# Program order for three engines, borders of stages written out, and six raw weight buffers in a two-layer encoder trunk

## The chip, the cores and the metric

The kernel runs on one core of a Trainium2 chip. The metric is the device time of one execution in microseconds (us); lower is better. Before the change it is 979.01 us, the median of three runs (977.41 to 979.86).

The engines named below are TensorE (PE: matrix products and transposes), VectorE (DVE), ScalarE (ACT), GpSimd (POOL) and SyncE (SP, which here only starts transfers). Each has its own instruction stream; they meet through semaphores.

## The reference, cut to what matters

x is 256 tokens by 1024 features, all in float32. Two layers run one after the other, each with a gated feed-forward block (FFN1), a mixing block ("mix") and a second feed-forward block (FFN2):

```
for l in range(DEPTH):                                   # DEPTH = 2, D_FF = 2816
    x = x + 0.5 * swiglu(rms_norm(x, ffn1_norm[l]), ffn1_w_gate[l], ffn1_w_up[l], ffn1_w_down[l])
    h = rms_norm(x, mix_norm[l])
    qa, ka, va, qb, kb, vb = split(h @ w_in[l])
    out_a = windowed_gqa_sink(qa, ka, va, sink[l], slopes_a)          # 8 heads, window 128
    lam   = exp(sum(lam_q1[l]*lam_k1[l])) - exp(sum(lam_q2[l]*lam_k2[l])) + lam_init
    out_b = rms_norm(differential_attention(qb, kb, vb, lam, slopes_b), diff_subln[l]) * (1 - lam_init)
    x = x + concat([out_a, out_b]) @ w_out[l]
    x = x + 0.5 * swiglu(rms_norm(x, ffn2_norm[l]), ffn2_w_gate[l], ffn2_w_up[l], ffn2_w_down[l])
return rms_norm(x, final_norm)
# swiglu(h, wg, wu, wd) = (silu(h @ wg) * (h @ wu)) @ wd
```

All weights are read from memory once, 167.5 MB in all.

## The kernel before, in words

*Products.* Every float32 product is made of three matmuls in a reduced 32-bit format (fp32r): each operand is split into a high part, rounded to fp32r, and a low part, the rest. The product is xh·whi + xl·whi + xh·wlo, added up in PSUM. `tokens` does this with 128 tokens as the stationary and 512 weight columns as the moving operand (128x512); `narrow` does it with the weights stationary and all 256 tokens moving (128x256).

*Weights.* `specs` is the list of all weight pieces in the order of use, mostly 1 MB each (128 partitions x 4 x 512). `emit_load` makes for one of them the transfer into a raw buffer on SP's queue, the casts on ACT (`whi`, L116) and the differences on DVE (`wlo`, L117). There are three buffers each of raw, whi and wlo. `weights()` hands out the next split weight and emits the loads up to two weights ahead (LOOK = 2); transfer and split of a weight are emitted together, and a transfer waits until the DVE difference that last read its raw buffer is done. The first two weights (gate and up, rows 0 to 511) come in four pieces each. `fine` marks the weights whose splits are cut in four.

*The order of work.* Instructions are emitted in Python in some order, and a scheduler (which plans with a timeline of its own) places them on each engine. PE's matmuls and transposes go through `mm` (L67) and `flip` (L70), which keep them in program order. ACT and DVE are in the scheduler's order, with `urgent()` raising the priority of norm operands, SiLU, the up product, splits of the hidden state and residual adds.

*Norms.* `Norm.pair(j)` transposes two 128-column blocks of x for both token halves (PE, four transposes of 128x128 for each block pair), and `operands` multiplies by the gain and splits the result: high part on ACT (L197), low part on DVE (L198), two of each per pair. `squares` sums x² on ACT (L183); `stats` makes r = 1/rms on DVE and POOL (L204 to L208); r is applied behind the products. The first FFN takes x by `take_x`, the later ones by `Residual.late`, which does what is left of the norm (pairs 2 and 3, squares, stats) inside the first matmul group of the next stage.

*FFN.* The 2816 hidden columns are five groups of 512 and one of 256. One group is: gate products in two halves of the features (k0 = 0, 4), up products in two halves, `hidden` (SiLU on ACT, L402; product with up on DVE, L408), `turn` (transposes of the hidden state of the group before and their split, ACT L336 and DVE L337), and two down products into accumulators that stay in PSUM for the whole FFN. In a full group PE does 144 matmuls of 128x512. `ffn_close` ends an FFN: the last down products are ordered so that columns 0 to 511 are complete first, are added to x (`Residual.add`, L382) and turned for the next norm, while columns 512 to 1023 are still being multiplied.

*Mix.* `first_groups` makes the keys and queries, which is the start of the input projection. Attention follows (lines 540 to 700), then the output projection: `out_part(w, k0, h)` takes two 128-row pieces of w_out from k0 on for column half h. Rows 4 to 7 belong to the differential attention (`oT[2:4]`, split in L682 and L683), rows 0 to 3 to the windowed attention, whose outputs are scaled on DVE (L702) and then transposed and split.

*Constants.* POOL starts the small transfers: the gains of the first norm (`grow1`, L225), then in `attention_constants` the other gains (L278, L279), after an iota and memsets the sinks (L299) and the four lambda vectors (L308), each copied to all 128 partitions. SP's queue starts with the first weights, ACT's with x in four pieces (L228).

Of the kernel before, what the change touches and what calls it, by code (L numbers as in the profile page):

```python
# [27 lines left out]
LOOK = 2  # L28
N_RAW, N_HI, N_LO = 3, 3, 3
N_S4 = 18  # L30
# [3 lines left out]
def trunk(ctx: ExitStack, tc: tile.TileContext, x, n1, g1, u1, d1, nm, w_in, sink,  # L34
          lq1, lk1, lq2, lk2, subln, w_out, n2, g2, u2, d2, nf, out):
    nc = tc.nc
    pe, act, dve, pool, sp = nc.tensor, nc.scalar, nc.vector, nc.gpsimd, nc.sync
# [27 lines left out]
    def mm(*a, **k):  # L65

        tc.keep_in_program_order(pe.matmul(*a, **k))  # L67

    def flip(*a):
        tc.keep_in_program_order(pe.transpose(*a))  # L70

# [4 lines left out]

    specs = []
    loaded = {}
# [7 lines left out]
    def plain(w, c0, n, k0=0, kn=None):  # L86
        src = rows(w, c0, n, k0, kn)
        kn = src.shape[1]
        return (kn, n, lambda t: [(t, src)])

    def emit_load(i):
        kn, n, moves = specs[i]
        raw = wp.tile([P, kn, n], F32, tag="raw", bufs=N_RAW, name=nm_("raw"))
# [4 lines left out]
        for dst, src in moves(raw):  # L98
            if i > 1:
                sp.dma_start(dst, src)  # L100
            else:
                for a, b in zip(cuts, cuts[1:]):
                    sp.dma_start(dst[:, a:b], src[:, a:b])  # L103
                    yield
# [15 lines left out]
    nxt = [0, 0]  # L120

    def weights():
        i = nxt[0]
        nxt[0] += 1
        while i > 1 and nxt[1] <= min(i + LOOK, len(specs) - 1):
            for _ in emit_load(nxt[1]):
                pass
            nxt[1] += 1
        return loaded.pop(i)

    for l in range(DEPTH):
        def ffn_specs(wg, wu, wd):
# [3 lines left out]
            for g in range(1, NGRP):  # L136
                specs.extend(plain(w[l], g * 512, 512, k0, 4) for w in (wg, wu) for k0 in (0, 4))
                specs.extend(down(g - 1, h) for h in range(2))
            for k0 in (0, 4):
                def gu_moves(t, k0=k0, ws=(wg[l], wu[l])):  # L140
                    return [(t[:, :, h * 256:h * 256 + 256], rows(w, FF - 256, 256, k0, 4)) for h, w in enumerate(ws)]
                specs.append((4, 512, gu_moves))
# [10 lines left out]
        for c in range(2):  # L153
# [3 lines left out]
            specs.append((KC, 256, qa_moves))  # L157
# [5 lines left out]
        for k0 in (0, 2):  # L163
# [3 lines left out]
            specs.append((2, D, o_moves))  # L167
# [6 lines left out]
    class Norm:  # L174


        def __init__(self, g0):
            self.g0, self.xs = g0, []
            self.ss = tmp("nss", 2, (P, 2, 4))

        def squares(self, t, c, n):
            j_ = tmp("junk", 2, (P, 512))
            act.activation(j_[:, :n], xk[:, t, c:c + n], AF.Square, accum_out=self.ss[:, t, c // 256:c // 256 + 1])  # L183

        def pair(self, j):
            sl = halves(bank())
            for i in range(2):
                for t in range(2):
                    flip(sl[:, i, t * P:(t + 1) * P], xk[:, t, (2 * j + i) * P:(2 * j + i + 1) * P], ident)
            with urgent():  # L190
                self.operands(j, sl)

        def operands(self, j, sl):
            xs = blk()
            for i in range(2):
                g = gcol[:, self.g0 + 2 * j + i:self.g0 + 2 * j + i + 1]
                self.last_act = act.activation(xs[:, i, 0:S], sl[:, i], AF.Identity, scale=g)  # L197
                self.last = dve.scalar_tensor_tensor(xs[:, i, S:512], in0=sl[:, i], scalar=g, in1=f(xs[:, i, 0:S]),  # L198
                                                     op0=ALU.mult, op1=ALU.subtract)
            self.xs.append(xs)  # L200
# [11 lines left out]
        def spread(self, sl):  # L212
# [4 lines left out]
            mm(sl[:, 0:S], lhsT=ones, rhs=dg, start=True, stop=True)  # L217
# [7 lines left out]
    pool.dma_start(grow1, n1.rearrange("l (k p) -> (l k) p", p=P))  # L225
    early = [emit_load(0), emit_load(1)]
# [4 lines left out]
    nxt[1] = 2  # L231
# [13 lines left out]
    def take_x(k):  # L245

        if k < 4:
            norm.pair(k)
            for e in early * 2 if k < 2 else ():
                next(e)  # L250
        else:
            with tc.issue_after(norm.last_act.ins):
                for t in range(2):
                    for h in range(2):
                        norm.squares(t, h * 512, 512)
            norm.stats()

    grow = const.tile([NG - 16, P], F32, name="grow")
    dist_i = const.tile([P, 512], mybir.dt.int32, name="dist_i")
# [7 lines left out]
    lin = const.tile([P, 4, DEPTH * 64], F32, name="lin")  # L267
    lsum = const.tile([P, 2, DEPTH], F32, name="lsum")
    lpr = const.tile([P, 2, DEPTH * 64], F32, name="lpr")
# [5 lines left out]

    def attention_constants():
        for i, g in enumerate((nm, n2)):
            pool.dma_start(grow[i * 16:(i + 1) * 16], g.rearrange("l (k p) -> (l k) p", p=P))  # L278
        pool.dma_start(grow[32:34], subln)  # L279
# [3 lines left out]

        pool.iota(dist_i, pattern=[[P, 2], [-1, S]], base=0, channel_multiplier=1)
        dflat = distB.rearrange("p a b -> p (a b)")
        aflat = distA.rearrange("p a b -> p (a b)")
        dve.tensor_copy(aflat, dist_i)
# [3 lines left out]


        for c in range(4):
            pool.memset(qscA[0:64, c:c + 1], -0.125 / slopeA[c])
            pool.memset(qscA[64:128, c:c + 1], -0.125 / slopeA[c + 4])
            pool.memset(qscB[:, c:c + 1], -0.125 / slopeB[c])


        pool.dma_start(snk_in, sink.rearrange("l h -> (l h)").partition_broadcast(P))  # L299
        sv = snk_in.rearrange("p (l s c) -> p l c s", l=DEPTH, s=2)  # L300
        for t in range(2):
            for l in range(DEPTH):
                pool.tensor_copy(snk[:, l, :, t, :], sv[:, l])
# [522 lines left out]
```

## Time and profile before

| | us |
|---|---|
| median of 3 runs | 979.01 |
| the profiled execution | 977.06 |
| its span, first to last instruction | 975.3 |
| PE busy | 954.0 |
| DVE busy | 555.4 |
| ACT busy | 475.1 |
| POOL busy | 22.0 |
| granted TensorE clock, mean | 0.998 |
| DMA rate over the span | 173 GB/s |

All durations below come from the one profiled execution. Its own time, 977.06 us, is 1.7 us more than its span and 1.95 us less than the median. The stages follow one another in the span: FFN1 of layer 0 from 0 to about 201 us, mix to 301, FFN2 to 490, FFN1 of layer 1 to 678, mix to 778, FFN2 to 968, and the final norm to 975. "Busy" counts the time in which an instruction of the engine runs; matmuls overlap, so a row of the timeline gives starts, and the distance from start to start is what a matmul costs. In such a row the first number is the start, the second the time to the end of the group, then engine, line and operation, what it writes and reads, its shapes, how many in a row, and in brackets how long the engine was idle before it and who ended that.

### The profile page before, as it was taken

The page shows a single profiled execution, that of the slowest core. Times are in us where ns is not written, and L with a number is a line of the kernel's source. Part 1 is how long each engine was busy: PE and PEld are TensorE (multiplying, and loading weights), DVE is VectorE, ACT ScalarE, POOL GpSimd, SP SyncE. Part 2 cuts the span into 40 slices and gives each one's busy share as a digit, 9 for nine tenths or more (in the row PEclk, how much of TensorE's full clock was granted, in tenths as well). Part 3 has the DMA queues.
Part 4 walks back from the last instruction along what each step waited for, and adds up shares of the span by engine and source line. Part 5 has one row for each costly group of instructions (what it writes and reads, how often), then busy time and mean ns, then how long its engine had stood idle before and what let it go on. Part 6 is the DMA issues. An engine that isn't in the chain of part 4 may idle for free.

```text
span 975.3 us, 12345 instructions
## 1 busy us (share of the span) xinstructions
PE 954.0 (98%) x4940; PEld 808.2 (83%) x4940; DVE 555.4 (57%) x850; ACT 475.1 (49%) x779; POOL 22.0 (2%) x50
## 2 busy tenths in 40 slices
PE   7999999999999999999999999999999999999997
PEld 5788888899897888888888888888999878888886
DVE  4755455569955554454565454456797455554453
ACT  5643443458834543434464443436576454434433
POOL 4000000000000000000000000000000000000001
PEclk9999999999999999999999999999999999999999
DMA  9655565545523655555555555555553246565531
GB/s 275 228 199 173 180 208 173 185 149 179 137 87 130 215 173 183 200 179 194 193 174 175 191 196 176 200 184 173 174 148 112 87 173 197 191 202 202 179 130 43
DMA packets 98217, 169.38 MB, mean 174 GB/s; under 512 B 3182, under 2 KB 30896, under 8 KB 98160
## 3 DMA queue, kind: packets, MB, share of 16 engines
q1 hardware_dynamic: 96784, 167.26, 52.4%
q0 software_dynamic: 288, 0.30, 0.4%
q10 hardware_dynamic: 1088, 1.05, 0.3%
q8 instruction: 38, 0.62, 0.3%
q14 instruction: 19, 0.16, 0.0%
HBM read 167.54 MB, written 1.05 MB: 173 GB/s over the span
## 4 chain that ended last, share of the span: by engine, by line
PE 93%; DVE 3%; DMA 2%; issue 1%; ACT 0%; SPq 0%; POOLq 0%; POOL 0%
PE ps L67 85%; PE ps L70 3%; DMA raw<-in_ffn_w_gate_dram 2%; DVE wlo L117 2%; PE ps L547 1%; PE ps L612 1%; PE ps L633 1%; PE ps L635 1%; PE ps L634 1%; PE ps L652 1%; DVE s L198 1%; DVE xk L382 0%; ACT whi L116 0%; ACT s L197 0%; SPq L103 0%
## 5 line engine op out<-in xcount | busy, mean ns | idle before, releaser
L67 PE MATMUL ps<-whi,s 128*128 128x512 f32 (+1 forms) x2252 | 697.9, 391 | 7.4 <-DVE s L198 5.6
L117 DVE TENSOR_TENSOR wlo<-raw,whi 128x1024 fp32r<-128x1024 f32 (+2 forms) x392 | 379.5, 1014 | 322.6 <-ACT whi L116 320.5
L67 PEld LDWEIGHTS ps<-whi,s 128*128 128x128 f32 x2252 | 420.1, 188 | 96.4 <-DVE s L198 8.2
L116 ACT CAST whi<-raw 128x1024 fp32r<-128x1024 f32 (+2 forms) x392 | 323.8, 882 | 344.0 <-PE ps L67 299.1
L67 PE MATMUL ps<-wlo,s 128*128 128x512 f32 (+1 forms) x1126 | 437.8, 389 | 0.0
L67 PEld LDWEIGHTS ps<-wlo,s 128*128 128x128 f32 x1126 | 211.7, 188 | 43.5
L67 PE MATMUL ps<-s,whi 128*128 128x256 f32 x448 | 82.7, 286 | 0.4 <-DVE s L198 0.4
L67 PEld LDWEIGHTS ps<-s,whi 128*128 128x128 f32 x448 | 70.1, 192 | 1.6 <-DVE s L198 0.8
L67 PE MATMUL ps<-s,wlo 128*128 128x256 f32 x224 | 63.3, 283 | 0.0
L402 ACT ACTIVATE tmp<-ps,r 128x512 f32<-128x512 f32 (+1 forms) x48 | 31.2, 651 | 61.7 <-PE ps L67 61.7
L408 DVE SCALAR_TENSOR_TENSOR s<-ps,hr,tmp 128x512 f32<-128x512 f32 (+1 forms) x48 | 32.7, 705 | 36.9 <-PE ps L67 27.4
L67 PEld LDWEIGHTS ps<-s,wlo 128*128 128x128 f32 x224 | 42.9, 192 | 0.0
L557 ACT ACTIVATE s<-s,negm 128x256 f32<-128x256 f32 x64 | 31.8, 498 | 9.6 <-DVE negm L555 9.6
L337 DVE TENSOR_TENSOR s<-ps,s 128x512 fp32r<-128x512 f32 x48 | 31.0, 683 | 6.1 <-ACT s L336 6.1
L197 ACT ACTIVATE s<-ps,gcol 128x256 fp32r<-128x256 f32 x48 | 21.7, 472 | 21.9 <-PE ps L70 19.0
L336 ACT CAST s<-ps 128x512 fp32r<-128x512 f32 x48 | 25.8, 583 | 9.5 <-PE ps L70 9.5
L198 DVE SCALAR_TENSOR_TENSOR s<-ps,gcol,s 128x256 fp32r<-128x256 f32 x48 | 22.2, 480 | 11.0 <-ACT s L197 10.6
L70 PE MATMUL ps<-ident,s 128*128 128x128 f32 x208 | 27.3, 272 | 0.0
L70 PEld LDWEIGHTS ps<-ident,s 128*128 128x128 f32 x208 | 24.3, 141 | 3.3
L183 ACT ACTIVATE junk<-xk 128x512 f32<-128x512 f32 x24 | 15.0, 627 | 14.2 <-DVE xk L382 14.2
L208 POOL TENSOR_TENSOR r<-ms,mhalf 128x2 f32<-128x2 f32 x6 | 4.2, 705 | 628.1 <-DVE ms L206 628.1
L382 DVE TENSOR_TENSOR xk<-xk,ps 128x512 f32<-128x512 f32 x20 | 13.6, 681 | 3.8 <-PE ps L67 3.8
(109 smaller groups left out, 347.4 us busy)
## 6 DMA issues: line engine op xcount, KB each, us to landing
raw<-in_ffn_w_down_dram SPq DMA_DIRECT2D x44, 1024.0 KB, 4.9
raw<-in_ffn_w_gate_dram SPq DMA_DIRECT2D x39, 1024.0 KB, 5.0
raw<-in_ffn_w_up_dram SPq DMA_DIRECT2D x39, 1024.0 KB, 5.0
raw<-in_w_in_dram SPq DMA_DIRECT2D x14, 1024.0 KB, 5.1
raw<-in_ffn_w_gate_dram SPq DMA_DIRECT2D x8, 512.0 KB, 3.6
raw<-in_ffn_w_up_dram SPq DMA_DIRECT2D x8, 512.0 KB, 4.6
raw<-in_w_in_dram SPq DMA_DIRECT2D x8, 512.0 KB, 4.4
raw<-in_w_out_dram SPq DMA_DIRECT2D x4, 1024.0 KB, 4.7
```

The lines of the kernel that those rows point to most:

```text
L67: tc.keep_in_program_order(pe.matmul(*a, **k))
L70: tc.keep_in_program_order(pe.transpose(*a))
L116: act.copy(h_, r_)
L117: dve.tensor_tensor(l_, r_, f(h_), op=ALU.subtract)
L183: act.activation(j_[:, :n], xk[:, t, c:c + n], AF.Square, accum_out=self.ss[:, t, c // 256:c // 256 + 1])
L197: self.last_act = act.activation(xs[:, i, 0:S], sl[:, i], AF.Identity, scale=g)
L198: self.last = dve.scalar_tensor_tensor(xs[:, i, S:512], in0=sl[:, i], scalar=g, in1=f(xs[:, i, 0:S]), op0=ALU.mult, op1=ALU.subtract)
L336: act.copy(dst[:, :, 0:S], src)
L337: dve.tensor_tensor(dst[:, :, S:512], src, f(dst[:, :, 0:S]), op=ALU.subtract)
L402: act.activation(g[:, :n], acc, AF.Silu, scale=norm.r[:, t:t + 1])
L408: dve.scalar_tensor_tensor(h[:, t, :n], in0=acc, scalar=norm.hr[:, t:t + 1], in1=g, op0=ALU.mult, op1=ALU.mult)
L557: act.activation(e[:, t, c], e[:, t, c], AF.Exp, scale=-1.0, bias=negm[:, n:n + 1], accum_out=den[:, n:n + 1])
```

## The change

- `Kept` wraps the handles of PE, ACT and DVE: as long as `kept[0]` is true, every instruction emitted through them is kept in program order. `mix` sets it to false behind `first_groups` and to true again at the output projection. `mm` and `flip` are gone; `urgent()` stays in one place of the attention.
- Raw buffers go from 3 to 6. `emit_load` becomes `emit_dma` and `emit_split`; `ahead(n)` emits splits up to weight n and transfers up to eight weights ahead as long as a raw buffer is free. `weights(look)` takes the distance of the split as an argument, 2 or, at three places, 1.
- `Step`, `seven`, `prod`, `by_seven`, `make_sums`, `quarter` and `summed` add a second way to do a group's gate and up products. `SEVEN` is empty, so none of it is emitted.
- The transfer of the first gains moves from POOL's queue to the head of SP's. POOL starts all its small transfers, sinks and lambda vectors among them, before the iota and the memsets; the latter and POOL's few operations on the constants follow.
- `take_x` interleaves the first pairs and the pieces of the first weights in a written order.
- `make_lam` becomes part of `attention_constants`, which runs ahead of group 3 of the first FFN. Three constants become blocks of the pool `s4`, which goes from 18 to 16 blocks.
- In a group, SiLU is emitted behind the gate products and ahead of the up products, and `turn` in the middle of the gate products in every group (before: in group 1 alone, else ahead of them).
- In `ffn_close`, pairs 0 and 1 are turned one matmul group earlier, the squares of columns 0 to 511 follow them, and then comes an explicit `ahead`. In `Residual.late` pairs 2 and 3 and squares come in one step, then the stats.
- In the output projection the weights are taken in the order 4, 6, 0, 2 with both column halves each; the first residual adds are cut into 256 columns, and the last four matmul groups alternate with pairs 0 and 1.

PE has the same number of instructions (4844). DVE has four more (the half adds), ACT two more table loads, SP one transfer more and POOL one less.

```diff
-LOOK = 2
-N_RAW, N_HI, N_LO = 3, 3, 3
-N_S4 = 18
+LOOK, AHEAD = 2, 8
+N_RAW, N_HI, N_LO = 6, 3, 3
+N_S4 = 16
+SEVEN = ()
...
+            def call(*a, **k):
+                ins = issue(*a, **k)
+                if kept[0]:
+                    tc.keep_in_program_order(ins)
+                return ins
...
+    at = dict(use=0, dma=2, prep=2, split=2)
+
+    def ahead(n):
+
+        n = min(n, len(specs) - 1)
+        while True:
+            if at["split"] <= n and at["prep"] > at["split"]:
+                for _ in emit_split(at["split"]):
+                    pass
+                at["split"] += 1
...
+            elif at["dma"] < min(at["use"] + AHEAD, len(specs)) and (specs[at["dma"]].moves is None or len(raws) < N_RAW):
+                if specs[at["dma"]].moves is not None:
+                    for _ in emit_dma(at["dma"]):
+                        pass
+                at["dma"] += 1
+            else:
+                break
+
+    def weights(look=LOOK):
+        i = at["use"]
+        at["use"] += 1
+        if i > 1:
+            ahead(i + look)
         return loaded.pop(i)
...
-    pool.dma_start(grow1, n1.rearrange("l (k p) -> (l k) p", p=P))
+    sp.dma_start(grow1, n1.rearrange("l (k p) -> (l k) p", p=P))
...
     def take_x(k):
 
+        g, u = early
+        if k == 0:
+            for j in (0, 1):
+                sl = norm.turn(j)
+                next(g)
+                norm.operands(j, sl)
+                next(u)
+        elif k == 1:
+            for e in (g, u, g, u):
                 next(e)
+            norm.pair(2)
+            ahead(2)
+            norm.pair(3)
+        elif k == 2:
+            ahead(3)
...
         def late(self, k):
 
-            if k == 2:
-                self.turn(1)
-            elif k == 3:
+            if k == 1:
+                self.nxt.pair(2)
+                self.nxt.pair(3)
+                self.squares(1)
+            elif k == 2:
                 self.nxt.stats()
...
-        group(1, [(k, t) for k in (1, 2) for t in range(2)])
-        res.turn(0)
+        group(1, [(1, t) for t in range(2)])
+        for j in range(2):
+            nxt.pair(j)
+        res.squares(0)
+        group(1, [(2, t) for t in range(2)])
+        ahead(at["use"] + LOOK - 1)
         group(1, [(3, t) for t in range(2)])
         for t in range(2):
             res.add(1, t)
...
-        w = weights()
-        for h in range(2):
-            out_part(w, 6, h)
-        ws = [weights(), weights()]
-        out_part(ws[0], 0, 0)
-        out_part(ws[1], 2, 0, BY_TOKENS)
-        for t in range(2):
-            res.add(0, t)
-        out_part(ws[0], 0, 1)
-        res.turn(0)
-        out_part(ws[1], 2, 1, BY_TOKENS)
+        for k0 in (6, 0):
+            w = weights()
+            for h in range(2):
+                out_part(w, k0, h)
+        w = weights()
+        out_part(w, 2, 0, BY_TOKENS)
+        for c in range(2):
+            for t in range(2):
+                res.add(0, t, c)
+        out_part(w, 2, 1, [(0, 0), (1, 0)])
+        nxt_norm.pair(0)
+        out_part(w, 2, 1, [(0, 1)])
+        nxt_norm.pair(1)
+        out_part(w, 2, 1, [(1, 1)])
+        res.squares(0)
         for t in range(2):
             res.add(1, t)
```

More of the change, by code (lines that the diff above doesn't have):

```diff
@@ L411, in hidden, with prod @@
+        def hidden(g, us):
             h = blk(F32)
             for t in range(2):
-                up(h, us[t], gate(gs[t], t), t)
+                up(h, us[t], g[t], t)
+            return h
+        def prod(xo):
+            hi, lo = weights()
+            acc = bank()
+            for k in range(4):
+                xh, xl = xo(k)
+                pe.matmul(acc, lhsT=xh, rhs=hi[:, k], start=k == 0, stop=False)
+                pe.matmul(acc, lhsT=xl, rhs=hi[:, k], start=False, stop=False)
+                pe.matmul(acc, lhsT=xh, rhs=lo[:, k], start=False, stop=k == 3)
+            return acc
@@ L459, in ffn @@
                 tokens(us, norm.xs, weights(), k0)
[L460 removed]
+            h = hidden(g, us)
             for hh in range(2):
[L462 to L465 removed]
+                down(hT, n - 1, hh, weights())
+        gu = [bank(), bank()]
+        tokens(gu, norm.xs, weights(), 0)
         hT = turn(h, 2)
[L468 to L471 removed]
+        tokens(gu, norm.xs, weights(), 4)
+        h = hidden(gate([b[:, 0:256] for b in gu]), [b[:, 256:512] for b in gu])
         return accs, hT, lambda: turn(h, 1)
```

362 lines of the change are left out of this document (232 added, 130 removed).

## The prediction

> **What bounds the kernel now.** I read the engine shares first, then the chain that ended last, then the matmuls one by one.
>
> ```profile
> PE 954.0 (98%) x4940; PEld 808.2 (83%) x4940; DVE 555.4 (57%) x850; ACT 475.1 (49%) x779; POOL 22.0 (2%) x50
> PEclk9999999999999999999999999999999999999999
> PE 93%; DVE 3%; DMA 2%; issue 1%; ACT 0%; SPq 0%; POOLq 0%; POOL 0%
> ```
>
> TensorE (PE) is busy 98% of the span at full clock, and the change leaves it the same 4844 instructions. A 128x512 matmul starts 0.227 us after the one before it, a 128x256 one 0.120, a transpose 0.109. With these paces the work between the first and last matmul (6.4 to 968.2 us) is 943.0 us, so only 961.8 − 943.0 = 18.8 us are there to be won, and anything the change adds is a new hole between matmuls. The holes, found as starts that come later than the pace, lie in few places: 7.0 us before 30 us, 3.1 at each border from the attention layer ("mix") to FFN2 (302 and 779 us), 0.56 at each border from FFN1 to mix (201 and 678), the rest small switches. Three spots of the timeline show the kinds:
>
> ```profile
> 6.41 0.26 PE L240 MATMUL ps<-ident,grow 16*128 16x16 f32 x1 [6.41 <-DMA grow<-in_ffn_norm_dram]
> 8.27 1.31 PE L67 MATMUL ps<-whi,s 128*128 128x512 f32 x2
> 19.36 2.18 ACT L116 CAST whi<-raw 128x512 fp32r<-128x512 f32 x4 [4.90 <-DMA raw<-in_ffn_w_gate_dram]
> ```
>
> PE begins only when the first norm gains (grow) land, runs its first matmuls at 0.43 us instead of 0.227, and after 21 us stands because the third weight, asked for at 7.04, landed at 19.33. The second kind, at the mix-to-FFN2 border, in the chain of waits and then the timeline:
>
> ```profile
> 298.73 1.06 ACT whi L116
> ...
> 299.81 2.36 DVE wlo L117 x2
> 302.17 0.43 DVE xk L382
> ...
> 302.69 0.87 DVE s L198 x2
> 303.56 0.59 DVE xk L382
> 304.15 2.27 DVE wlo L117 x2
> 306.42 0.41 DVE s L198
> ```
> ```profile
> 303.22 0.50 PE L67 MATMUL ps<-whi,s 128*128 128x512 f32 x1 [0.49 <-DVE s L198]
> 305.39 0.50 PE L67 MATMUL ps<-whi,s 128*128 128x512 f32 x1 [0.72 <-ACT s L197]
> 306.87 0.50 PE L67 MATMUL ps<-whi,s 128*128 128x512 f32 x1 [0.98 <-DVE s L198]
> ```
>
> VectorE (DVE) runs weight differences (wlo, L117) between the residual adds (L382) and the norm operands (L198) for which PE waits: what DVE and ScalarE (ACT) do in which order sets the end here, and that order is what the change writes out.
>
> **The change part by part.**
>
> *Start.* SyncE (SP), not GpSimd (POOL), asks for the gains: on SP its DMA goes ahead of the weights at some 0.7 us instead of 1.29. The weight pieces asked for at 0.72 and 1.17 land at 4.04 and 5.34, so the gains land by 3.5 to 5, and the first x piece (4.67) becomes what PE waits for. First matmul at 6.2 to 7.0 instead of 8.27. With six raw buffers the four 1 MB loads that were asked for at 7.04, 13.06, 15.21 and 22.53, the last three when a buffer came free, are asked for one behind the other by about 9.5. x, the eight first pieces and the third load are 4.2 MB, 11 us at the 366 to 388 GB/s of the windows from 4 to 10 us; from 2 us on, and with some 4 us lost in the low stretch told below, the third load lands at 17 to 18, the next two some 2.7 us of bytes apart, at 20 and 22.5. Then the wait at 21 us and the holes behind it go. From the paces, of the 7.0 us before 30 us about 5.9 to 7.0 go; I take −6.3. Against it: the broadcast loads of sinks and lambdas (L299, L308) are asked for by POOL at 3.1 to 5.9 instead of 5.95 to 8.7. While they run the windows of 2 us show 226, 178 and 129 GB/s (10 to 16 us) between 383 and 362 before and after. So the low stretch moves onto the first pieces and may cost what it costs now one load later: two to three pieces 1 to 3 us late. Bounds −8 (PE runs as soon as x lands) and −3 (only the gains' 1.7 us and part of the third load's wait). The Trainium skill ("DMA: Bandwidth & Descriptors", Queues, rings and completion order) says that each DMA engine takes its queues in turn, a packet at a time, so POOL's small packets hold up SP's loads. The windows agree. By that rule alone the pieces run at a half of their rate for some 4 us, 2 us late, and the sum would be 2 higher.
>
> *FFN groups.* 20 full groups of 33 us, and four halves. ACT and DVE in program order: per group six casts of 1 MB (2 x 1.0 us each), two SiLU (0.65), two hidden-state splits (0.58); DVE six differences (2 x 1.18), two products (0.70), two splits (0.68). ACT 14.5 us, DVE 16.9 of 33.6. Walking the new order along PE's times, each split is ready over 6 us before PE reads it and SiLU and product follow their last matmul at once. The cover is these 6 us: 0, bounds 0 and +0.1 a group (a switch of 0.1 as in the attention), +2 in all.
>
> *FFN1 to mix, twice.* Now the scheduler put the cast of the second projection weight at 196.12, into ACT's idle time:
>
> ```profile
> 196.12 2.00 ACT L116 CAST whi<-raw 128x1024 fp32r<-128x1024 f32 x2 [1.09 <-issue]
> 199.47 1.50 ACT L197 ACTIVATE s<-ps,gcol 128x256 fp32r<-128x256 f32 x3 [1.34 <-PE ps L70]
> ```
>
> In the new text that split stands behind the norm operands of pairs 0 and 1 and two squares. Pairs come one group of matmuls earlier, ACT has four L197 (0.47) from about 197.7, each second one held by a DVE L198, then squares (1.23): the cast ends at about 203.3, while PE reads that weight at 202.5: hole 0.8; its difference 1.18 later at 0.227 us cover: 0.95; then DVE has the second half (1.18) and two adds (0.68 each) before pair 2's operands: about 1.25. Together 3.0 against 0.56: +2.4 each, +4.8. Bounds 0 (the squares slip into waits) and +4 each (PE also waits for the pairs).
>
> *FFN2 of layer 0 to FFN1 of layer 1, once.* Same text, but weights of 1 MB that PE eats in 5.4 us: +0.5, bounds 0 and +1.5.
>
> *Mix to FFN2, twice.* The adds are cut to 256 columns, pair 0 is turned behind the halves it needs, the operand groups alternate with matmuls, and all weight splits stand before or behind them. DVE's 2.36 and 2.27 us of wlo leave the chain shown above. By the rows (a 128x256 add 0.42 as in L761, L197 0.47, L198 0.48) a hole of 0.3 stays of 2.8: −2.5 each, −5.0; bounds −2.8 and 0 each.
>
> *Entry of the output projection, twice.* PE's transposes of the diff-attention output are now in a fixed place with less behind them: before, 24 value matmuls, 8 transposes and 8 more (1.77 us) covered the operands; now 30, 2, 1, 6, 1. In the fixed DVE order the scaling of the second head block (L702, 0.69) comes ahead of the two splits (L683, 0.70). PE's second matmul needs the low half: about 1.2 late, +2.3 for two; bounds 0 and +2 each.
>
> *The rest.* In the attention PE's order changes in the score blocks only (+0.3, switches of 0.16). The lambda work moves into the third group of the first FFN and loads two more ACT tables (1.28 each): hidden in the 19 us of a group in which ACT is idle; uncovered, 2.6. Two tiles fewer in the s4 pool: no wait seen for one. The tail from the last matmul (7 us) is untouched.
>
> Sum: −6.3 + 0 + 4.8 + 0.5 − 5.0 + 2.3 + 0.3 = −3.4. The profiled execution took 977.06 us (span 975.3), 1.95 under the median of 979.01; I take the difference over: 979.0 − 3.4 = 975.6.
>
> **The rivals.**
>
> *A. The start collides (slower).* Place: 4 to 14 us, POOL's broadcasts against the first eight pieces. For it: the three low windows and pieces like u3 that took 7.7 us (6.11 to 13.81). Against: they carry only 0.3 MB. Price: the matmuls that read u3 begin near 20, so its 3 us are covered; the third load isn't. Landing 3 us later than now, at 22.3, it lets PE go on at 25 instead of 21.96, the gains' head start is eaten by that wait, and only the later hole of 1.7 behind 27.15 goes with the six buffers: start 3.0 − 1.7, about +1.5 instead of −6.3, sum +4.4: 983.4. It decides once the third weight's cast starts later than 22 us (now 19.36).
>
> *B. The start gains little.* The third load lands at 19.3 as now, since eight pieces and x are ahead of it in the same 16 engines; only the gains' 1.7 us and some of the second-group holes are won: start −4.5, or −3 with the slow first matmuls; sum −1.6 to −0.1. With −1.6: 977.4.
>
> *C. The FFN-to-mix holes don't open.* ACT sits idle 1 to 3 us in these stretches, and my hand order may be too strict: −3.4 − 4.8 = −8.2: 970.8.
>
> *D. Program order costs in every FFN group.* Each engine now waits at an instruction whose matmuls aren't done while later casts could run; 0.5 us, as long as the holes at 303 us, in 20 groups gives +10, less 3.4: 985.6. Against it: DVE's idle time is 322.6 us in front of wlo alone and PE shows no hole inside a group.
>
> *E. The clock.* PE's first matmuls are slow (0.43) until 11.1 and fast from then. If earlier but thinner work at the start keeps holes, it stays slow: 0.2 us for each matmul, 30 of them +6: sum +2.6, 981.6. The Trainium skill ("TensorE: Matmul & The Clock Gate", Part 1) halves the clock after about 3.4 us of idling and wants that long of work to warm; the trace agrees as far as holes of 1.25 us at 306 us left 0.227 behind them.
>
> **How the numbers follow.** What this kernel's measurement can tell from no change is 0.3%, 2.9 us. Forecast 0.40 (its own range 973 to 978), B 0.20, C 0.13, A 0.12, D 0.08, E 0.07. The gate for faster is 976.1, so the forecast gives 0.28 faster and 0.12 same; B 0.06 and 0.14, since its start may yet be better than −4.5; C is faster; A and D are slower; E 0.04 same, 0.03 slower. Faster 0.28 + 0.06 + 0.13 = 0.47, same 0.12 + 0.14 + 0.04 = 0.30, slower 0.12 + 0.08 + 0.03 = 0.23. Range: from C's 970.8, less 1.3 for a start nearer its bound, to A's 983.4, rounded: 969.5 to 983.5. It leaves out D and the far ends.
>
> **What would show it.** Right: first matmul before 7.5 us, no hole over 0.5 us from 19 to 30; at 300 us (shifted by 6) no wlo between adds and operands; at the FFN-to-mix border three holes near 0.8, 0.95 and 1.25 with ACT's second-weight cast behind the squares; a hole of 1.2 on DVE's L683 at the output projection's entry; unchanged 33 us per group. Wrong: holes repeating every 33 us (D), matmuls at 0.43 beyond 15 us (E), the third cast after 22 us (A).

## The result and the profile after

The changed kernel takes 976.01 us (median of 13 runs, 975.56 to 977.90); the kernel before, run beside it, 979.01 us (13 runs, 976.87 to 982.26). The ratio is 0.997, 95% interval 0.9958 to 0.9981: 3.0 us faster. The profiled execution took 975.68 us, with a span of 973.9.

The engine shares on the page of the changed kernel. All instructions made through `Kept` carry its line, L50, so they are told apart by tiles.

```profile
PE 956.1 (98%) x4940; PEld 807.9 (83%) x4940; DVE 558.7 (57%) x854; ACT 479.0 (49%) x781; POOL 20.2 (2%) x49
```

TensorE (PE) bounds the kernel as before, with the same number of instructions: both pages count 4940 (the 4844 named further up stands on neither). Between the profiled executions the change is 975.68 − 977.06 = −1.4 us, less than half of what the medians show; why they differ is told below. Comparing the start of the n-th PE instruction in the two traces (called PE's starts below) shows where these 1.4 us lie:

| place | after minus before, us | this stage's share | forecast |
|---|---|---|---|
| behind the first FFN group (start) | −4.30 | −4.3 | −6.3 |
| end of the full FFN groups of layer 0 | −4.24 | +0.1 | 0 |
| behind FFN1 to mix | −1.76 | +2.5 | +2.4 |
| end of attention | −1.34 | +0.4 | +0.15 |
| behind the entry of the output projection | +0.01 | +1.35 | +1.15 |
| behind mix to FFN2 | −3.05 | −3.1 | −2.5 |
| behind FFN2 to FFN1 of layer 1 | −2.54 | +0.5 | +0.5 |
| behind FFN1 to mix, layer 1 | −0.03 | +2.5 | +2.4 |
| end of attention | +0.38 | +0.4 | +0.15 |
| behind the entry of the output projection | +1.73 | +1.35 | +1.15 |
| behind mix to FFN2 | −1.30 | −3.0 | −2.5 |
| end of the span | −1.4 | −0.1 | 0 |

*The start*, PE and then ScalarE (ACT) in the timeline of the changed kernel:

```profile
3.65 1.11 PE L50 MATMUL ps<-ident,xk 128*128 128x128 f32 x4 [0.30 <-DMA xk<-in_x_dram]
6.01 1.20 PE L50 MATMUL ps<-whi,s 128*128 128x512 f32 x2
12.69 0.73 PE L50 MATMUL ps<-whi,s 128*128 128x512 f32 x2 [0.57 <-ACT whi L50]
15.77 0.73 PE L50 MATMUL ps<-whi,s 128*128 128x512 f32 x2 [0.28 <-ACT whi L50]
```
```profile
12.03 0.62 ACT L50 CAST whi<-raw 128x512 fp32r<-128x512 f32 x1 [1.61 <-DMA raw<-in_ffn_w_up_dram]
15.10 0.62 ACT L50 CAST whi<-raw 128x512 fp32r<-128x512 f32 x1 [2.46 <-DMA raw<-in_ffn_w_gate_dram]
17.95 0.47 ACT L50 ACTIVATE s<-ps,gcol 128x256 fp32r<-128x256 f32 x1
20.14 2.19 ACT L50 CAST whi<-raw 128x512 fp32r<-128x512 f32 x4 [0.46 <-DMA raw<-in_ffn_w_gate_dram]
```

PE's first product begins 2.3 us earlier (6.01 instead of 8.27), then PE stands for weight pieces that land at 12.00 and 15.07. By 21 us the lead is down to 0.2. Then it grows to 4.3, because the holes that the kernel before has from 21 to 29 us aren't there. The third weight doesn't come earlier: it landed at 20.11, before the change at 19.33. What differs is what stands behind it on ACT. Before, the cast that waits for this load (19.36, shown in the prediction) had the operands of pair 2 behind it, though pair 2 had been transposed at 15.34. ACT in the kernel before:

```profile
21.44 0.47 ACT L197 ACTIVATE s<-ps,gcol 128x256 fp32r<-128x256 f32 x1
```

Now the operands (17.95) come first.

*FFN1 to mix*, PE, then ACT, then VectorE (DVE):

```profile
199.14 0.50 PE L50 MATMUL ps<-s,whi 128*128 128x256 f32 x2 [0.69 <-ACT whi L50]
200.40 0.39 PE L50 MATMUL ps<-s,wlo 128*128 128x256 f32 x1 [0.76 <-DVE wlo L50]
202.13 0.33 PE L50 MATMUL ps<-ident,xk 128*128 128x128 f32 x1 [0.28 <-DVE xk L50]
202.73 0.98 PE L50 MATMUL ps<-ident,xk 128*128 128x128 f32 x7 [0.27 <-DVE xk L50]
```
```profile
193.87 0.47 ACT L50 ACTIVATE s<-ps,gcol 128x256 fp32r<-128x256 f32 x1 [6.83 <-PE ps L50]
...
198.06 4.06 ACT L50 CAST whi<-raw 128x1024 fp32r<-128x1024 f32 x6
```
```profile
199.12 2.36 DVE L50 TENSOR_TENSOR wlo<-raw,whi 128x1024 fp32r<-128x1024 f32 x2 [1.82 <-ACT whi L50]
201.40 1.28 DVE L50 TENSOR_TENSOR xk<-xk,ps 128x512 f32<-128x512 f32 x2
```

ACT idles 6.83 us ahead of the pairs, and the cast that PE needs next waits behind pairs and squares until 198.06. PE waits for the cast, then for its difference, then for the two residual adds behind that. The excess, the time by which matmuls start later than PE's pace, is 0.85 + 0.92 + 0.44 + 0.49 = 2.7 us against 0.56 before.

*Mix to FFN2*, DVE and then PE:

```profile
297.06 2.36 DVE L50 TENSOR_TENSOR wlo<-raw,whi 128x1024 fp32r<-128x1024 f32 x2 [3.04 <-ACT whi L50]
299.34 1.41 DVE L50 TENSOR_TENSOR xk<-xk,ps 128x256 f32<-128x256 f32 x4
```
```profile
300.08 0.60 PE L50 MATMUL ps<-ident,xk 128*128 128x128 f32 x4
300.44 0.71 PE L50 MATMUL ps<-whi,s 128*128 128x512 f32 x2
```

The weight difference lies ahead of the adds, the first half adds release the transposes in time, and no PE row here shows a wait. The 3.1 us of holes are gone.

*The entry of the output projection*, DVE and PE of the changed kernel, then PE of the kernel before:

```profile
277.46 0.69 DVE L50 TENSOR_TENSOR s<-ps,ra 128x512 f32<-128x512 f32 x1 [2.72 <-PE ps L50]
278.07 1.40 DVE L50 SCALAR_TENSOR_TENSOR s<-ps,gsub,s 128x512 fp32r<-128x512 f32 x2
```
```profile
277.09 0.33 PE L50 MATMUL ps<-vA,s 128*128 128x64 f32 x2
277.76 0.50 PE L50 MATMUL ps<-whi,s 128*128 128x512 f32 x1 [0.34 <-ACT s L50]
278.87 0.50 PE L50 MATMUL ps<-whi,s 128*128 128x512 f32 x1 [0.60 <-DVE s L50]
```
```profile
276.92 1.90 PE L67 MATMUL ps<-vA,s 128*128 128x64 f32 x16
278.62 0.72 PE L67 MATMUL ps<-whi,s 128*128 128x512 f32 x2
```

The scaling of the windowed output (read from `ps,ra`) runs ahead of the low halves that PE's second matmul needs; the excess is 0.50 + 0.88 us. Before, 16 value products stood between the transposes and the projection, and it began without a wait.

### The profile page after: what moved, and what is told of

Read it like the earlier page. It is cut to its first block, busy times and chain, and to the rows that moved or that the text cites. A ratio compares the mean times of both kernels' runs of the same rounds, so it can differ in the third digit from the quotient of the medians.

```text
span 973.9 us, 12341 instructions
## 1 busy us (share of the span) xinstructions
PE 956.1 (98%) x4940; PEld 807.9 (83%) x4940; DVE 558.7 (57%) x854; ACT 479.0 (49%) x781; POOL 20.2 (2%) x49
## 4 chain that ended last, share of the span: by engine, by line
PE 94%; DVE 2%; DMA 1%; ACT 1%; issue 1%; POOLq 0%; POOL 0%; SPq 0%
PE ps L50 94%; DMA raw<-in_ffn_w_gate_dram 1%; DVE s L50 1%; DVE wlo L50 1%; ACT s L50 0%; ACT whi L50 0%; DVE xk L50 0%; DMA xk<-in_x_dram 0%; ACT junk L50 0%; ACT tmp L50 0%; POOLq L1018 0%; POOL rf L968 0%; DVE rf L50 0%; SPq L162 0%
## 5 line engine op out<-in xcount | busy, mean ns | idle before, releaser
L50 PE MATMUL ps<-whi,s 128*128 128x512 f32 (+1 forms) x2316 | 718.3, 391 | 2.8 <-DVE s L50 1.2
L50 DVE TENSOR_TENSOR wlo<-raw,whi 128x1024 fp32r<-128x1024 f32 (+2 forms) x392 | 378.5, 1014 | 229.8 <-ACT whi L50 225.9
L50 PEld LDWEIGHTS ps<-whi,s 128*128 128x128 f32 x2316 | 431.2, 188 | 91.7 <-ACT whi L50 2.3
L50 PE MATMUL ps<-wlo,s 128*128 128x512 f32 x1158 | 450.8, 389 | 0.2 <-DVE wlo L50 0.2
L50 ACT CAST whi<-raw 128x1024 fp32r<-128x1024 f32 (+2 forms) x392 | 323.1, 884 | 244.9 <-PE ps L50 222.0
L50 PEld LDWEIGHTS ps<-wlo,s 128*128 128x128 f32 x1158 | 217.7, 188 | 47.1 <-DVE wlo L50 2.3
L50 PE MATMUL ps<-s,whi 128*128 128x256 f32 x448 | 83.1, 286 | 1.4 <-ACT whi L50 1.4
L50 PEld LDWEIGHTS ps<-s,whi 128*128 128x128 f32 x448 | 70.1, 192 | 2.8 <-ACT whi L50 1.8
L50 ACT CAST s<-ps 128x512 fp32r<-128x512 f32 x48 | 26.0, 589 | 94.2 <-PE ps L50 94.2
L50 DVE TENSOR_TENSOR s<-ps,s 128x512 fp32r<-128x512 f32 x48 | 31.1, 687 | 71.6 <-ACT s L50 71.6
L50 PE MATMUL ps<-s,wlo 128*128 128x256 f32 x224 | 63.5, 284 | 1.5 <-DVE wlo L50 1.5
L50 ACT ACTIVATE tmp<-ps,r 128x512 f32<-128x512 f32 (+1 forms) x48 | 30.8, 654 | 45.6 <-PE ps L50 45.6
L50 DVE SCALAR_TENSOR_TENSOR s<-ps,hr,tmp 128x512 f32<-128x512 f32 (+1 forms) x48 | 32.4, 706 | 31.8 <-PE ps L50 25.4
L50 ACT ACTIVATE s<-ps,gcol 128x256 fp32r<-128x256 f32 x48 | 21.6, 472 | 51.0 <-PE ps L50 33.1
L50 PEld LDWEIGHTS ps<-s,wlo 128*128 128x128 f32 x224 | 42.9, 192 | 1.9 <-DVE wlo L50 1.9
L50 PE MATMUL ps<-ident,s 128*128 128x128 f32 x304 | 39.9, 273 | 0.0
L50 PEld LDWEIGHTS ps<-ident,s 128*128 128x128 f32 x304 | 35.1, 141 | 4.7
L50 DVE SCALAR_TENSOR_TENSOR s<-ps,gcol,s 128x256 fp32r<-128x256 f32 x48 | 22.3, 482 | 28.2 <-ACT s L50 28.2
L50 ACT ACTIVATE s<-s,negm 128x256 f32<-128x256 f32 x64 | 31.9, 500 | 7.4 <-DVE negm L50 7.4
L50 PE MATMUL ps<-ident,xk 128*128 128x128 f32 x96 | 14.5, 288 | 1.9 <-DVE xk L50 1.1
L50 PEld LDWEIGHTS ps<-ident,xk 128*128 128x128 f32 x96 | 11.6, 146 | 4.7 <-DVE xk L50 1.9
```

What stands on the lines that cost most here:

```text
L50: ins = issue(*a, **k)
```

## The experiments

Twelve kernels were run, each with five rounds beside the kernel before, whose medians in these jobs were 979.57, 980.12 and 979.35 us. e1 to e4 share the first job, e5, e7, e8 and e9 the second, e6, e10, e11 and e12 the third; below they are ordered by question. Ratios are against the kernel before in the same job.

### Do the small broadcasts hold up the start?

e1 puts the broadcasts of the changed kernel behind the first FFN's r.

```diff
-    pool.dma_start(snk_in, sink.rearrange("l h -> (l h)").partition_broadcast(P))
-    for i, a in enumerate((lq1, lk1, lq2, lk2)):
-        pool.dma_start(lin[:, i], a.rearrange("l d -> (l d)").partition_broadcast(P))
...
+            with tc.issue_after(norm.powed.ins):
+                sinks_and_lambdas()
```

> The changed kernel with the loads of the sinks and lambda vectors (five transfers copied to 128 partitions) and the POOL work on them started behind the first FFN's r, near 30 us, instead of at 3.45 to 5.64 us. Theory: their small packets share the 16 engines with SP's first weight pieces; without them the rate stays near 360 to 390 GB/s between 8 and 14 us instead of 186, 129 and 187, the fourth piece lands near 9 instead of 12.0 and the fifth near 10 instead of 15.07, PE's holes of 0.73 at 11.7 and 0.44 at 15.2 go, and the time is 1.2 to 2.5 us less than the changed kernel's 976.0: about 974. Rival: the pieces are late because SP asks for them late (3.63 and 4.00) and x lies ahead of them; then the rate and the landings stay within 1 us of what they are and the time is 976.

Measured: 974.21 us (973.68 to 976.25), ratio 0.995 (0.9932 to 0.9967). The page's DMA part restricted to 8 to 14 us, first of the changed kernel, then of e1: the rate, and the queues by packets, MB and share of the 16 engines' time (q0 carries POOL's transfers, q1 SP's; the shares add up packet times, which overlap, and can pass 100%).

```profile
DMA packets 559, 1.01 MB, mean 168 GB/s; under 512 B 115, under 2 KB 141, under 8 KB 559
...
q0 software_dynamic: 149, 0.26, 61.5%
q1 hardware_dynamic: 393, 0.73, 38.9%
```
```profile
DMA packets 1256, 2.33 MB, mean 389 GB/s; under 512 B 102, under 2 KB 132, under 8 KB 1256
...
q1 hardware_dynamic: 1216, 2.30, 103.4%
```

A quarter of a megabyte takes 61.5% of the engines for 6 us and leaves the weights a third of their rate. Without it the fourth piece lands at 10.23 instead of 12.00, the fifth at 10.90 instead of 15.07, and the holes at 11.7 and 15.2 us are gone. Against this, PE waits longer for x's second piece (landed at 6.58 instead of 5.20), a hole of 2.03 us; by PE's starts 1.5 us are won in all. The theory holds, but for the word small: of the 61.5%, 59.8 are 63 packets of 4096 bytes that take 0.91 us each, where SP's of 2048 bytes take 0.10. By their bytes (64 in all, four times 64 KB) they are the four lambda vectors'. Packets of 512 bytes or less take 1.7%. The Trainium skill ("DMA: Bandwidth & Descriptors", Queues, rings and completion order) has each engine take its queues in turn, a packet at a time. That POOL's packets hold up SP's agrees with the shares; whether the turns go one for one the counts (149 and 393) don't show. Why these packets take 0.91 us stays open.

e8 does the same to the kernel before: its `attention_constants` loses the five broadcasts, which go to the same place.

> The kernel before the change with the sinks' and lambda vectors' loads and POOL's work on them behind the first FFN's r, near 30 us, as in the run of the changed kernel with late broadcasts. Theory: in both kernels the runs differ from one another by the start alone, by how late the first weight pieces land and whether PE then stands long enough to be slow again; without these loads the median falls by 1.5 to 3 us from the 979.6 of its neighbour to 977 and below, and the runs lie within 2 us of one another instead of 4.9, with a granted clock of 0.997 or more. Rival: the spread has another source (the loads of 1 MB or the clock by itself): median 979 to 980, spread over 4 us, clocks of 0.994 among the runs.

Measured: 973.06 us (972.78 to 976.09), ratio 0.9945 (0.9927 to 0.9964). By the medians the old kernel with this one edit is 7.1 us faster than without, where 1.5 to 3 were expected. Between the profiled runs (977.06 and 972.86) it is 4.2, all of it before 30 us. The rest comes from runs of the kernel before that are slower and have a lower granted clock; the last section shows how a late piece does this in other kernels (a slow start, below). Four of six runs lie within 0.35 us; two are at 976.0 and 976.1 with a granted clock of 0.994, so the spread (3.3 us, 5.0 in its neighbour) is smaller but not gone. In its trace the third weight lands at 14.55 instead of 19.33, and of the excess from 20 to 30 us 0.7 of 4.5 us is left. So an early load closes these holes as well as the new order does.

With the broadcasts late in both, nothing is left of the change's gain: e1's 974.21 against e8's 973.06, 974.27 against 972.86 for the profiled runs. By PE's starts the change then wins 1.6 us at the start instead of 4.3, and loses the same 3 us at the other places together.

### Do six buffers or the early gains win the start?

e5 and e12 set `N_RAW` back to 3, in the changed kernel and in e1; e6 and e11 give the gains back to POOL, in the same two.

```diff
-N_RAW, N_HI, N_LO = 6, 3, 3
+N_RAW, N_HI, N_LO = 3, 3, 3
...
-    sp.dma_start(grow1, n1.rearrange("l (k p) -> (l k) p", p=P))
+    pool.dma_start(grow1, n1.rearrange("l (k p) -> (l k) p", p=P))
```

> The changed kernel with three raw buffers instead of six, nothing else. Theory: the six buffers act at the start alone, by asking for the third to sixth load before 13.1 us; with three these loads wait for VectorE's differences again, PE stands behind them before 35 us, and the time is 2 to 4 us more than the changed kernel's 976.0: 978 to 980, with the border from mix to FFN2 closed as it is (under 0.3 us). Rival: the early loads are what closes that border; then holes of over 1 us come back at 300 and 777 us and the time is above 980.

> The changed kernel with late broadcasts and three raw buffers. Theory: as with early broadcasts, the loads that six buffers ask for early aren't what PE waits for; the place of pairs 2 and 3 ahead of the third weight's split is; 974.2 within 0.5. Rival: with PE 1.8 us ahead the fourth to sixth load become what it waits for: 975.5 or more, with holes between 20 and 35 us.

> The changed kernel with the first gains (grow1) asked for on POOL's queue again. Theory: PE's first transposes come 2 to 3 us later (near 6.3 instead of 3.65), but PE stands for the fourth and fifth weight piece at 11.7 and 15.2 us anyway, so little of it arrives: 976.0 to 976.8. Rival: the move of the gains is what won the start; then 977.7 or more.

> The changed kernel with late broadcasts and the first gains on POOL's queue. Theory: with the broadcasts out of the way nothing stands behind the first matmul that hides the gains; it comes at 8.3 instead of 7.4 us, and the time is 974.2 + 0.9 = 975.1, up to 1.5 more. Rival: x's second piece (6.6 us) is what PE waits for in both; 974.2 within 0.4.

| run | us (range) | ratio |
|---|---|---|
| e5, three buffers | 976.46 (975.78 to 978.71) | 0.9969 (0.9958 to 0.9981) |
| e12, late broadcasts, three buffers | 973.91 (973.80 to 974.07) | 0.9941 (0.9926 to 0.9955) |
| e6, gains on POOL | 976.06 (975.30 to 976.73) | 0.9962 (0.9947 to 0.9976) |
| e11, late broadcasts, gains on POOL | 975.72 (975.16 to 976.35) | 0.9960 (0.9945 to 0.9975) |

Six buffers are worth nothing measurable, at the start or at the borders; e5's expectation of 2 to 4 us fell, and its border from mix to FFN2 is as closed. The other three expectations held. The early gains are worth nothing while PE waits for pieces anyway, and 1.5 us once it doesn't (975.72 against e1's 974.21; in the same job e12 has 973.91). By PE's starts the two profiled runs differ by 0.9. What is left for the start's win is the written order of the first pairs and casts. This was not undone by itself, so it stands by the rows at 17.95 and 20.14 and by exclusion: in e5 and e6 too the third weight lands late, at 20.0 and 20.1, and no hole follows up to 30 us. e4, told next, tests it in part. There the scheduler puts one operand of pair 2 on ACT behind the waiting cast, at 23.38, and a hole of 0.62 us follows at 25.28.

### Where do the borders come from?

e2 moves one line in the changed kernel:

```diff
         tail(1)
+        ahead(at["use"] + LOOK - 1)
         group(1, [(1, t) for t in range(2)])
...
-        ahead(at["use"] + LOOK - 1)
         group(1, [(3, t) for t in range(2)])
```

> The changed kernel with one call moved: at the end of an FFN the split of the second weight of the next stage is emitted ahead of the group before pairs 0 and 1, not behind the squares. Theory: the holes at the border from FFN1 to mix (0.85, 0.92, 0.44 and 0.49 us at 198 to 202 us, the same at 677 to 681) come from that place alone; ACT is idle for 6.8 us ahead of the pairs, the cast fits there, the border costs 0.2 to 0.6 instead of 2.7, and the time falls by 4 to 5 (and 0.4 more at the border from FFN2 to FFN1): about 971.3. Rival: the split then delays the operands of pairs 0 and 1 by its 2.4 us of DVE and the holes move to the pairs: within 1.5 us of 976.

Measured: 971.51 us (970.10 to 973.56), ratio 0.9921 (0.9903 to 0.9939). In its trace no hole over 0.15 us is left at these borders. The theory holds, and the place of one split costs the changed kernel 4.5 us by the median. By PE's starts it is more, 2.95 at each border from FFN1 to mix and 0.5 from FFN2 to FFN1, 6.4 in all. The median falls short because some runs have slow starts, the profiled one (973.56) among them; the three at a clock of 0.998 or 0.999 take 970.10 to 970.69.

e4 leaves ACT and DVE to the scheduler everywhere:

```diff
-    pe, act, dve = Kept(nc.tensor), Kept(nc.scalar), Kept(nc.vector)
+    pe, act, dve = Kept(nc.tensor), nc.scalar, nc.vector
```

> The changed kernel with ACT and DVE left to the scheduler everywhere, PE as in the changed kernel; text, buffers and transfers unchanged. Theory (program order is what closes and opens the holes): the border from mix to FFN2 opens again by 1 to 3 us each, the one from FFN1 to mix closes by about 2.5 each, the start worsens by 0 to 2 as casts run ahead of norm operands: 974 to 978. Rival (the text and the buffers matter, the kept order doesn't): all holes stay where they are, 976 within 0.7.

Measured: 972.81 us (972.27 to 974.39), ratio 0.9935 (0.9919 to 0.9950): 3.2 us faster than the changed kernel, which neither theory allowed. The border from FFN1 to mix closes (one hole of 0.18 each); in its trace the start costs 2.0 us more. The border from mix to FFN2 stays nearly closed: by PE's starts it costs 0.56 us more than in the changed kernel. So the kept order of ACT and DVE gave 0.56 of the 3.05 us won there, and the new text the rest, with the half adds and pairs between matmuls and the weights' order 4, 6, 0, 2. Which of these did it no run separates; e5 excludes the buffers.

### The entry of the output projection, and the sum

e3 keeps PE in program order in the attention as well:

```diff
-                if kept[0]:
+                if kept[0] or self.always:
...
-    pe, act, dve = Kept(nc.tensor), Kept(nc.scalar), Kept(nc.vector)
+    pe, act, dve = Kept(nc.tensor, True), Kept(nc.scalar), Kept(nc.vector)
```

> The changed kernel with PE kept in program order in the attention too, as it was before the change; ACT and DVE stay with the scheduler there. Theory: the 1.4 us at the entry of the output projection come from PE's order (2 transposes, 2 value matmuls, 6 transposes where there were 8 transposes and 8 value matmuls behind them), and with the order of before 1.2 to 1.4 come back at each entry and 0.3 to 0.4 in each attention: 972.5 to 973. Rival: DVE's order decides (the scaling of the value product ahead of the two low halves) and stays: within 0.7 us of 976.

Measured: 975.07 us (974.42 to 978.51), ratio 0.9959 (0.9947 to 0.9972). The entry closes, with no PE row waiting there, but the scheduler's new order of ACT and DVE opens holes of 0.7, 0.2 and 0.3 us in each attention. By PE's starts 1.35 us come back at each entry and 0.45 are lost in each attention, 1.8 in all; by the medians only 0.9 us arrives where 3 were expected. The profiled run had a slow start.

e7 is e1, e2 and e3 together; e9 is e1, e3 and e4 together; e10 is e7 with PE kept only from the windowed value products on.

```diff
-                if kept[0]:
+                if kept[self.flag]:
...
-    pe, act, dve = Kept(nc.tensor), Kept(nc.scalar), Kept(nc.vector)
+    pe, act, dve = Kept(nc.tensor, 1), Kept(nc.scalar), Kept(nc.vector)
...
-        kept[0] = False
+        kept[:] = [False, False]
...
+        kept[1] = True
         oa = [bank() for _ in range(2)]
```

> The changed kernel with three edits together: broadcasts late, the second weight's split ahead of the pairs at the end of an FFN, and PE kept in program order in the attention. Theory: the three act in different stages and add up, 976.0 - 1.8 - 4.5 - 0.9 = 968.8, within 1.0. Rival: the time saved at one place is waited for at the next, since the weights' transfers set a pace (167.5 MB at 174 GB/s); then no more than the largest, 971.5.

> The changed kernel with ACT and DVE left to the scheduler everywhere, broadcasts late and PE kept in program order in the attention. Theory: the scheduler closes the border from FFN1 to mix by itself, so this comes out as the three edits with kept orders do, within 1.5 us: 972.8 - 1.8 - 0.9 = 970.1. Rival: with ACT and DVE free the holes at the entry of the output projection stay (VectorE's scaling ahead of the low halves), 971.5 to 972.5.

> The run of the three edits, but PE is kept in program order only from the windowed value products on; the scores and transposes ahead of them are in the scheduler's order as in the changed kernel. Theory: the entry of the output projection stays closed, and the holes of 0.7 and 0.5 us that the kept order opened in each attention (240 and 250 us, 715 and 726) go: 965.5 - 1.4 = 964.1, within 0.5. Rival: the two are one order, and the entry opens again: 966 to 968.

| run | us (range) | ratio |
|---|---|---|
| e7 | 965.47 (965.16 to 965.53) | 0.9858 (0.9839 to 0.9876) |
| e9 | 968.02 (967.87 to 969.49) | 0.9888 (0.9869 to 0.9907) |
| e10 | 964.57 (964.29 to 965.47) | 0.9847 (0.9829 to 0.9865) |

e7 came out 3.3 us under the sum of the three medians and e9 2.1 under its own, so both numbers were missed; that the places add up, and that the weights' transfers set no pace here, holds. By PE's starts e7 wins 2.0 us against the changed kernel at the start, 6.4 at the FFN's borders and 2.7 at the entries, and loses 0.9 in the attention, together −10.2; so do the two profiled runs (965.47 and 975.68), and the medians show −10.5. The medians of the parts fell short because some of their runs had slow starts. e9 closes the entry, but is 2.6 us slower than e7, outside the 1.5 expected: 0.7 at the start, 0.3 at each border from FFN1 to mix and 0.6 at each from mix to FFN2. So with that one split well placed, keeping ACT and DVE in program order wins over the scheduler, though the changed kernel lost to it. e10 is the best of all, 14.8 us under the kernel before, within 0.5 of its expectation, and closes the entry without the attention's holes; PE's rows there:

```profile
269.84 1.04 PE L50 MATMUL ps<-ident,s 128*128 128x128 f32 x8
270.72 1.90 PE L50 MATMUL ps<-vA,s 128*128 128x64 f32 x16
272.43 0.72 PE L50 MATMUL ps<-whi,s 128*128 128x512 f32 x2
```

Eight transposes, then 1.7 us of value products that cover the operands, then the projection without a wait. On DVE the second scaling now comes at 272.65, behind the two low halves (271.26), though DVE is left to the scheduler here.

## Why the prediction was right, and where it was not

The time, 976.01, is 0.4 us from the forecast, and the direction is right, but that it came so near is luck: the sum of −3.4 was 2.0 us too good for the profiled runs, and scatter of the kernel before made up 1.6.

*The carry from the profile to the median.* "I take the difference over" failed. Between profiled executions the change is −1.4 us, not −3.4. The rest of the median's −3.0 is scatter of the kernel before. Of its 17 runs in the second job three show 977.05 to 977.52 us at a granted clock of 0.998, five show 978.34 to 980.80 at 0.996, seven 979.28 to 980.67 at 0.994 and two 981.58 and 982.02 at 0.992. The profiled one was of the first kind. The changed kernel's runs are mostly of that kind (0.998 and 0.999 in 11 of 13). A change that evens out the start moves the median by more than a comparison of two good executions shows.

*Start (−6.3, measured −4.3).* The place was right, the working wrong. The first transposes do begin with x, at 3.65 us, but "the wait at 21 us and the holes behind it go" was laid to six buffers and an earlier third load. The load came later (20.11), and e5 shows the buffers to be worth nothing. The holes went, by the rows and by exclusion, since pair 2's operands no longer stand behind the cast that waits for it. This is rival B's start (−4.5, third load as before) for another reason, and for the profiled pair B's sum of −1.6 is the nearer number.

*Rival A* has its place and mechanism shown by e1 and e8, but not its price: the third cast started at 20.14, under the 22 us from which it would decide, and the broadcasts cost 1.8 us in the changed kernel and 7.1 in the one before (1.5 and 4.2 by PE's starts). Nor were the packets that cost it small. By the rule of the Trainium skill weighed in the forecast ("DMA: Bandwidth & Descriptors", Queues, rings and completion order, +2 us) the start would have been −4.3, as measured; the pieces did take 2.1 us of PE's lead by 21 us, but the −6.3 under it rested on the buffers, so the figure agrees in part by luck.

*FFN groups (0).* Right: the lead stays between 4.30 and 4.24 us from the second group to the border; rival D falls.

*FFN1 to mix (+2.4 each, measured +2.5), FFN2 to FFN1 (+0.5, +0.5).* Right in size and cause: the holes were forecast as 0.8, 0.95 and 1.25 and are 0.85, 0.92 and 0.93, and e2 removes them by the one line named. Rival C falls.

*Mix to FFN2 (−2.5 each, measured −3.1 and −3.0).* Right in kind; the 0.3 us left over for late operands was too careful. That it needs the kept order on ACT and DVE, as the reading of the chain suggested, is false by e4 for 2.5 of the 3.05 us.

*Entry of the output projection (+1.15 each, measured +1.35).* Right in place and size, wrong in what sets the order. The forecast speaks of a fixed place for PE's transposes and a fixed DVE order, but `kept[0]` is false until the output projection begins, so both come from the scheduler. What moved the transposes is that PE, kept in order there before the change, no longer is. e3 and e10 keep it again and the holes go; DVE's order follows, as e10's rows show.

*The rest (+0.3, measured +0.8).* The attention costs 0.4 more each time. PE's new order of the score blocks is the reason given; that it comes from switches of 0.16 us is not shown. With PE's order of before (e3) the attention is not faster but 0.45 slower still, as ACT's and DVE's order moves with it.

*Rival E* isn't the rule here, but it occurs, as the last section shows.

## What to carry to other kernels

Broadcasts of constants that nobody needs yet belong behind the first weights: 0.26 MB cost this kernel 4 us before the change and 1.5 after, and 7 and 2 by the medians. When an order is written by hand, look at each instruction that may wait for a transfer and ask which ready work stands behind it, and at each idle stretch of an engine for the split that could fill it; two such places decided +5.0 and some −4 us here. Whether the written order beat the scheduler hung on one misplaced split: 3.2 us slower with it, 2.6 faster without. And a sum made from one profiled execution predicts another profiled execution; where runs scatter by their start, the median can move by more.

## What the runs showed of the hardware

The scatter has a visible mechanism. In e2's profiled run the fourth weight piece landed at 14.88 us (9.45 to 10.23 in e1, e7, e9, e10 and e12, without broadcasts), PE stood from 12.2 to 15.6, and then ran at half speed. The windows of its trace, and then PE's rows:

```profile
12.00:16.00 4.00, 0.82 (x3) 0.43 (x2) 0.45 (x1) 0.74 (x2) 0.45 (x1) 0.85 0.94 223
16.00:20.00 4.00, 4.00 (x15) 3.27 (x14) 2.81 (x5) 2.73 (x5) 0.46 (x1) 0.50 1.04 392
20.00:24.00 4.00, 4.00 (x16) 3.23 (x16) 2.85 (x6) 2.79 (x6) 0.00 (x0) 0.80 1.05 387
```
```profile
15.57 1.22 PE L50 MATMUL ps<-whi,s 128*128 128x512 f32 x2 [3.18 <-ACT whi L50]
16.59 0.63 PE L50 MATMUL ps<-wlo,s 128*128 128x512 f32 x1
```

In a window's row the third number from the end is the granted TensorE clock: 0.85, 0.50, 0.80. Matmuls start 0.43 us apart instead of 0.227 until 21.3 us. e3's profiled run shows the same behind an excess of 4.0 us. Holes with an excess of 1.67 (e5) and 1.74 us (e4) at the same place left the clock full. The trace's clock record has one half from 14.81 to 21.64 in e2 and from 15.19 to 22.02 in e3. The Trainium skill ("TensorE: Matmul & The Clock Gate", Part 1) gives an idle window of about 3.4 us that halves the clock and about as much work to restore it. Holes of this length do halve it, but the figures differ: the clock fell 2.4 us (e2) and 3.1 us (e3) after PE's last matmul ended, and came back after 6.1 us of work. So a piece that lands 3 us late costs the hole and then some 3 us more. What makes the landing vary from run to run while the broadcasts are in flight, and why e8 still has two runs at 0.994, stays open. So does the slow start of the kernel before, since no such run of it was profiled; its clocks of 0.994 are those of e2 and e3 (0.994 and 0.995).
